# Seven block products for eight in the down projections and in five pairs of W_up columns of a two-layer encoder

## The chip, the cores and the metric

The kernel runs on one core of a Trainium2 chip. A core has TensorE (PE, matmuls; PEld is its weight load), VectorE (DVE), ScalarE (ACT), GpSimd (POOL), SyncE (SP, which issues most DMAs) and 16 DMA engines. Operands lie in SBUF with 128 partitions; matmuls add into PSUM, which has eight banks of 128 x 512 float32. Each engine works through its own instructions in order and waits on semaphores for others. The metric is the device time of one execution in microseconds (us).

## The reference

Two layers over x of 512 positions x 1024 channels, all in float32:

```
h   = RMSNorm(x);  p = h @ W_in            # Fourier group, q, k, v
x   = x + concat(RMSNorm(Fourier part), RMSNorm(windowed attention)) @ W_o
h   = RMSNorm(x)
up  = DWConv3_centred(h @ W_up)             # 2 x 2816 columns, 3 taps along positions, bias
x   = x + (silu(up[:, :2816]) * up[:, 2816:]) @ W_down
```

The last three lines are the ConvFFN, which the change rewrites. Its hidden width of 2816 is 22 blocks ("ff tiles") of 128.

## The kernel before

Channels lie on the partitions and the 512 positions on the free dimension, so x is eight tiles `x[0]` to `x[7]` of 128 x 512. Every operand of a matmul is split into a high part (`whi` for weights, written by ACT as a rounding copy) and a low part (`wlo`, written by DVE as the difference, L93). A product is three matmuls, high x high, low x high, high x low (`mm3`, L120 to L122), with a block of weights of 128 x 128 as the stationary operand and 512 positions as the moving one. `whi` and `wlo` have five buffers each, a raw weight tile (`wraw`) is loaded by SP.

The ConvFFN of a layer runs in two halves of 11 ff tiles (`HALVES`). For each ff tile the kernel makes two W_up tiles (gate and value): two weight splits of 512, 24 matmuls into one bank, then DVE multiplies the bank by the norm's factor (`tF<-ps,rb`), ACT takes the middle tap of the convolution, and DVE the two other taps (L96). ACT applies silu, and the gate's product is made on DVE in layer 0 and on POOL in layer 1; it is split into `gu`, held in buffers with the names slab, pT and m4. Then comes the down projection of the half: for each of the eight tiles of x 11 blocks x 3 matmuls of 512 into one bank, and one DVE addition x += bank. In the last half of layer 1 the last of the eight tiles is done in two pieces of 256 positions.

In layer 0's ConvFFN a generator (`presplit`) splits layer 1's remaining weights (44 pieces, of W_qkv, W_in, the Fourier weights and W_o) into high and low parts in `tA` buffers and stores them in DRAM (`kept`), from which layer 1 fetches them. `next(ahead)` in the loops lets it go on by one piece.

The code is written in the order of the computation; a scheduler that simulates the engines decides the order of the instructions on each engine when the program is built.

Of the kernel before, what the change touches and what calls it, by code (L numbers as in the profile page):

```python
# [37 lines left out]
def encoder_kernel(tc, t):
# [109 lines left out]

    def presplit(l):
# [15 lines left out]
        def cols(src, n, step):  # L165
            def load():
                raw = temp(1024, "m4")
                nc.sync.dma_start(raw[:, :n], src)
                return [raw[:, c:c + step] for c in range(0, n, step)]
            return load  # L170

        def prepare(kind, raw):
            if kind == "u":
                return fold_wu(raw)
            return fold_wf(raw) if kind == "f" else raw

        jobs = []
        for grp in (1, 0):
            for kk in range(KT // 2):
                jobs.append((cols(t["w_qkv"][l, grp, kk], 768, 384), [f"qkv{grp}{2 * kk + i}" for i in range(2)]))  # L180
        for kk in range(KT // 2):
            jobs.append((lambda kk=kk: load_wu(l, kk, temp(1024, "m4")), [f"u{2 * kk + i}" for i in range(2)]))
        for j in range(NF):
            jobs.append((lambda j=j: [load_wf(l, j, temp(1024, "m4"))], [f"f{j}"]))
        for half in range(2):
            for mp in range(KT // 2):
                jobs.append((cols(t["w_o"][l, half, :, mp * 1024:(mp + 1) * 1024], 1024, 512),
                             [f"o{half}{2 * mp + i}" for i in range(2)]))
        got = jobs[0][0]()
        for n, (_, keys) in enumerate(jobs):  # L190
            for i, key in enumerate(keys):
                keep(key, prepare(key[0], got[i]))
                if i == len(keys) - 1 and n + 1 < len(jobs):
                    got = jobs[n + 1][0]()
                yield
# [182 lines left out]
    for l in range(L):
# [325 lines left out]
        ahead = presplit(l + 1) if l < L - 1 else iter(lambda: 0, 1)  # L704
        for f0, nf in HALVES:
            gu = []
            for fi in range(f0, f0 + nf):
                ys_ = []
                n = fi - f0
                for z in range(2):  # L710
                    m = fi + z * FT
                    w = wchunks(t["w_up"][l, m], 1024)
                    nps[0] += 1
                    o = psum(FFN_BANKS[nps[0] % len(FFN_BANKS)])
                    for k in range(KT):
                        mm3(o, [q[:, (k % 4) * P:(k % 4 + 1) * P] for q in w[k // 4]], [h2[k][:, s, :] for s in range(2)],
                            k == 0, k == KT - 1)
                    u = temp(512, "tF")
                    tt(u, o, rb2, ALU.mult)
                    y = temp(512, "tF")  # L720
                    act(y, u, AF.Identity, scale=cw[:, l, 1, m:m + 1], bias=cb[:, l, m:m + 1])
                    stt(y[:, 1:], u[:, :-1], cw[:, l, 0, m:m + 1], y[:, 1:], ALU.mult, ALU.add)
                    stt(y[:, :-1], u[:, 1:], cw[:, l, 2, m:m + 1], y[:, :-1], ALU.mult, ALU.add)
                    ys_.append(y)
                    if (2 * n + z) % 3 == 2:
                        next(ahead)
                act(ys_[0], ys_[0], AF.Silu)
# [1 line left out]
                if n < 4:
                    a = pair("slab")  # L730
                elif n < 8:
                    if n % 2 == 0:
                        two = temp(2048, "pT", F32R).rearrange("p (n s q) -> p n s q", n=2, s=2)
                    a = two[:, n % 2]
                else:
                    a = pair("m4")
                split(a[:, 0, :], a[:, 1, :], ys_[0])
                gu.append(a)
            nxt = []
            for m in range(KT):  # L740
                next(ahead)
                next(ahead)
                w = []
                for c in range(0, nf, 8):
                    n = min(8, nf - c)
                    w += wchunks(t["w_down"][l, m, :, (f0 + c) * P:(f0 + c + n) * P], n * P)
                end = l == L - 1 and f0 + nf == FT
                nh = 2 if end and m == KT - 1 else 1
                for h in range(nh):
# [100 lines left out]
```

## Time and profile before

| | before |
|---|---|
| median of 3 runs | 1056.19 us (1055.73 to 1057.11) |
| the profiled execution | 1056.14 us, its span 1054.3 us, granted clock 0.999 |
| PE busy | 1038.2 us, 98% of the span |
| DVE busy | 726.8 us, 69% |
| ACT busy | 507.9 us, 48% |
| POOL busy | 90.8 us, 9% |
| ConvFFN of layer 0, 155 to 509 us | PE 354.00 of 354 us, DVE 264.77 |
| ConvFFN of layer 1, 685 to 1051 us | PE 366.00 of 366 us, DVE 236.50 |
| DMA | 140.03 MB, 133 GB/s in the mean |

An instruction's recorded duration is longer than its share of a busy engine, since neighbours overlap; the distance of two starts tells what one costs there. Releasers of waits are inferred from semaphore events.

### The profile page before, as it was taken

How to read it: one execution, taken by the hardware profiler on the slowest of the kernel's cores; microseconds unless marked ns; L12 is line 12 of the kernel's file. 1: busy time of each engine (PE TensorE's matmuls, PEld its weight loads, DVE VectorE, ACT ScalarE, POOL GpSimd, SP SyncE). 2: the span in 40 equal slices, each digit the busy share in tenths (PEclk: the TensorE clock that was granted, in tenths of full speed). 3: DMA queues.
4: the chain of work that ended last, by engine and by line, in shares of the span. 5: the costliest groups of instructions: out<-in, count | busy, mean ns of one | idle time of the engine just before them, and what ended most of it. 6: DMA issues, size and time to landing. Idle time of an engine off the chain costs nothing.

```text
span 1054.3 us, 14425 instructions
## 1 busy us (share of the span) xinstructions
PE 1038.2 (98%) x5107; PEld 873.2 (83%) x5107; DVE 726.8 (69%) x1384; ACT 507.9 (48%) x939; POOL 90.8 (9%) x164
## 2 busy tenths in 40 slices
PE   8998999999999999999999999999999999999998
PEld 8986778888888888888899887888888888888887
DVE  8878768697767777777519775478877336878632
ACT  5339755455444445455423785246554224454421
POOL 0004410000000000000000152001101000101100
PEclk9999999999999999999999999999999999999999
DMA  7232152332269833239856313333332333332241
GB/s 273 83 115 87 58 193 81 100 100 96 78 226 353 324 100 101 89 114 322 280 181 221 113 62 99 122 100 94 101 101 74 96 115 100 98 101 82 82 150 48
DMA packets 60475, 140.03 MB, mean 133 GB/s; under 512 B 6642, under 2 KB 22258, under 8 KB 60404
## 3 DMA queue, kind: packets, MB, share of 16 engines
q1 hardware_dynamic: 60404, 139.12, 40.5%
q8 instruction: 40, 0.66, 0.3%
q14 instruction: 31, 0.25, 0.1%
HBM read 116.02 MB, written 23.07 MB: 132 GB/s over the span
## 4 chain that ended last, share of the span: by engine, by line
PE 93%; DVE 2%; DMA 2%; ACT 1%; issue 1%; POOL 0%; SPq 0%; ACTq 0%; DVEq 0%; POOLq 0%
PE ps L122 28%; PE ps L120 28%; PE ps L121 28%; PE ps L118 3%; PE ps L548 2%; PE ps L541 2%; PE ps L529 1%; DMA wraw<-in_w_qkv_dram 1%; PE ps L234 1%; PE ps L227 1%; ACT tA L90 0%; DMA x<-in_xT_dram 0%; DVE tA L533 0%; ACT act L90 0%; PE ps L500 0%
## 5 line engine op out<-in xcount | busy, mean ns | idle before, releaser
L90 ACT ACTIVATE whi<-wraw 128x512 fp32r<-128x512 f32 (+1 forms) x296 | 182.0, 616 | 290.8 <-PE ps L122 278.4
L120 PE MATMUL ps<-act,whi 128*128 128x512 f32 x768 | 298.9, 390 | 0.0
L121 PE MATMUL ps<-act,wlo 128*128 128x512 f32 x768 | 298.3, 389 | 0.0
L122 PE MATMUL ps<-act,whi 128*128 128x512 f32 x768 | 298.2, 389 | 0.0
L93 DVE TENSOR_TENSOR wlo<-wraw,whi 128x512 fp32r<-128x512 f32 (+1 forms) x304 | 219.7, 726 | 103.4 <-ACT whi L90 102.0
L122 PEld LDWEIGHTS ps<-act,whi 128*128 128x128 f32 x768 | 144.2, 188 | 30.1
L120 PEld LDWEIGHTS ps<-act,whi 128*128 128x128 f32 x768 | 144.2, 188 | 29.7
L121 PEld LDWEIGHTS ps<-act,wlo 128*128 128x128 f32 x768 | 144.2, 188 | 29.7
L96 DVE SCALAR_TENSOR_TENSOR tF<-tF,pb,tF 128x511 f32<-128x511 f32 x176 | 133.5, 763 | 11.1 <-ACT tF L90 8.7
L93 DVE TENSOR_TENSOR tF<-ps,rb 128x512 f32<-128x512 f32 x104 | 71.2, 689 | 77.9 <-PE ps L122 64.7
L120 PE MATMUL ps<-slab,whi 128*128 128x512 f32 (+2 forms) x212 | 82.2, 388 | 0.0
L122 PE MATMUL ps<-slab,whi 128*128 128x512 f32 (+2 forms) x212 | 79.9, 380 | 0.4 <-DVE slab L93 0.3
L121 PE MATMUL ps<-slab,wlo 128*128 128x512 f32 (+2 forms) x212 | 80.0, 378 | 0.0
L90 ACT ACTIVATE tF<-tF,pb 128x512 f32<-128x512 f32 x88 | 71.7, 816 | 11.3 <-DVE tF L93 4.6
L93 DVE TENSOR_TENSOR x<-x,ps 128x512 f32<-128x512 f32 (+1 forms) x49 | 32.9, 674 | 36.5 <-PE ps L122 36.3
L93 POOL TENSOR_TENSOR tF<-tF,tF 128x512 f32<-128x512 f32 x22 | 30.2, 1371 | 256.1 <-DVE tF L96 224.1
L120 PE MATMUL ps<-pT,whi 128*128 128x512 f32 (+1 forms) x132 | 50.5, 383 | 0.0
L121 PE MATMUL ps<-pT,wlo 128*128 128x512 f32 (+1 forms) x132 | 50.5, 383 | 0.0
L122 PE MATMUL ps<-pT,whi 128*128 128x512 f32 (+1 forms) x132 | 50.5, 383 | 0.0
L538 POOL TENSOR_SCALAR tA<-tA,den 128x256 f32<-128x256 f32 (+1 forms) x64 | 37.4, 590 | 145.1 <-DVE den L537 144.6
L533 DVE CUSTOM_DVE_ANT_0 tA<-ps,pb,nsink 128x256 f32<-128x256 f32 (+1 forms) x64 | 37.8, 603 | 14.5 <-PE ps L529 9.7
L122 PEld LDWEIGHTS ps<-slab,whi 128*128 128x128 f32 x212 | 39.7, 188 | 8.3 <-DVE slab L93 0.9
(178 smaller groups left out, 1485.0 us busy)
## 6 DMA issues: line engine op xcount, KB each, us to landing
wraw<-in_w_up_dram SPq DMA_DIRECT2D x88, 512.0 KB, 3.5
wraw<-in_w_down_dram SPq DMA_DIRECT2D x32, 512.0 KB, 3.7
kept<-tA SPq DMA_DIRECT2D x56, 256.0 KB, 5.7
whi<-kept SPq DMA_DIRECT2D x28, 256.0 KB, 3.0
wlo<-kept SPq DMA_DIRECT2D x28, 256.0 KB, 3.0
kept<-tA SPq DMA_DIRECT2D x32, 192.0 KB, 4.4
wraw<-in_w_down_dram SPq DMA_DIRECT2D x32, 192.0 KB, 2.4
wraw<-in_w_o_dram SPq DMA_DIRECT2D x8, 512.0 KB, 3.7
```

The costliest lines, as they stand in the source:

```text
L90: return nc.scalar.activation(out, in_, func, **kw)
L93: return (eng or nc.vector).tensor_tensor(out, a, b, op=op)
L96: return nc.vector.scalar_tensor_tensor(out=out, in0=a, scalar=s, in1=b, op0=op0, op1=op1)
L118: nc.tensor.matmul(out, a[0], b[0], start=start, stop=stop, **kw)
L120: nc.tensor.matmul(out, a[0], b[0], start=start, stop=False, **kw)
L121: nc.tensor.matmul(out, a[1], b[0], start=False, stop=False, **kw)
L122: nc.tensor.matmul(out, a[0], b[1], start=False, stop=stop, **kw)
L227: nc.tensor.matmul(pt[:, 2 * b:2 * b + 2], acc[:, b * P:(b + 1) * P], ones2, start=True, stop=True)
L533: nc.vector.tensor_tensor_reduce(out=pr[:, :n], in0=sc[:, :n], in1=mask[:, m0:m0 + n], scale=qs_scale[p][:, i, e:e + 1], scalar=nsink[:, l ...
L538: nc.gpsimd.tensor_scalar(pr[:, :n], pr[:, :n], den[:, i:i + 1], 1.0, op0=ALU.mult, op1=ALU.mult)
L541: tr = nc.tensor.transpose(pp[:, j * P:(j + 1) * P], pr[:, j * P:(j + 1) * P], ident)
L548: pv = nc.tensor.matmul(py[64 * e:64 * e + 64, i0 * P:(i1 + 1) * P], vp[:, j, 64 * g:64 * g + 64], pT[:, half, e, b0:b0 + 2 * (i1 - i0) + ...
```

## The change

**Groups.** The ConvFFN of both layers runs in three groups of 6, 8 and 8 ff tiles (`GROUPS`) instead of two halves of 11.

**Down projection.** A pair of x tiles (rows 1 and 2 of a 2 x 2 block matrix) is made from two halves of the group's ff tiles (columns) and two halves of the 512 positions. Seven products of blocks take the place of eight. With A the weights and B the right operands, A's sums are S1 = A21 + A22, S3 = A11 - A21, S2 = S3 - A22, S4 = A12 + S2, and B's sums T1 to T4 (`sums_of_b`). Each product has kp blocks (3 or 4) x 3 matmuls of 256. They go to three banks: X gets B11, T2, T3 and T4 in turn, Y gets T1 and then B22, Z gets B21. A bank goes on adding; after each product DVE adds the whole bank to the part of x to which the sum so far belongs, and only then may the next product go on in the bank. The additions are seven of 256 a pair.

**Weight sums** are made by DVE (`wsum` in layer 0, `tA` in layer 1), except S1 of the first three pairs of a group, for which SP loads A21 and a DMA issued by POOL adds A22 to it (18 in all). All seven left operands of a pair are split into high and low parts.

**Right operands.** The ff tiles are made in the order in which the two of a pair follow each other. For a pair `seven_gu` makes four sums of 256 on DVE and splits 3.5 tiles of 512.

**W_up.** In layer 1 the pairs of W_up tiles with the numbers 4, 8, 11, 16 and 19 (`SEVEN`) are made by the same seven products (`up_seven`, 84 matmuls of 256 for 48 of 512), with sums of h2 that are made once (`seven_h`) in rooms that are free by then. Banks are read out between products by ACT and DVE.

**Others.** The gate's product is on DVE in both layers. The ConvFFN takes banks in a ring of eight (`BANKS8`) instead of six. `presplit` works in 44 jobs of one piece each; the high copies wait for the last convolution's first step (`pace`), and raw pieces lie in the `tail` buffers.

```diff
+GROUPS = [(0, 6), (6, 8), (14, 8)]
+SEVEN = ((), (4, 8, 11, 16, 19))
+BANKS8 = ("mm", "mm", "mm", "av", "sc", "sc", "tp", "tp")
...
         def keep(key, src):
             two = [temp(n, "tA", F32R) for _ in range(2)]
-            split(two[0], two[1], src)
+            with tc.issue_after(pace[0]):
+                act(two[0], src)
+            tt(two[1], src, f(two[0]), ALU.subtract)
...
+    def sums_of_b(b1, b2):
+        t13, t24 = temp(512, "tF"), temp(512, "tF")
+        tt(t13[:, LO], b1[:, HI], b1[:, LO], ALU.subtract)
+        tt(t13[:, HI], b2[:, HI], b1[:, HI], ALU.subtract)
+        tt(t24[:, LO], t13[:, LO], b2[:, HI], ALU.subtract)
+        tt(t24[:, HI], t24[:, LO], b2[:, LO], ALU.add)
+        return t13, t24
...
+    def seven_gu(b1, b2, room):
+        t13, t24 = sums_of_b(b1, b2)
+        one = next(room)
+        g = dict(B11=[one[:, LO], one[:, HI]])
+        split(*g["B11"], b1[:, LO])
+        parts(g, b2, ("B21", "B22"), room)
+        parts(g, t13, ("T1", "T3"), room)
+        parts(g, t24, ("T2", "T4"), room)
+        return g
...
+    def up_seven(l, fi, h2, ts, rb2):
...
+        product(X, wsplit(a11), "B11", True)
+        act(ua[:, LO], X)
+        s1, s2, s3, s4 = [temp(512, "tA") for _ in range(4)]
+        tt(s1, a21, a22, ALU.add)
+        product(Y, wsplit(s1), "T1", True)
+        act(ub[:, HI], Y)
+        product(Z, wsplit(a12), "B21", True)
+        tt(ua[:, LO], ua[:, LO], Z, ALU.add)
...
+        product(X, wsplit(s2), "T2")
+        act(ua[:, HI], X)
...
+        product(X, wsplit(a22), "T4")
...
+    def first_two(l, mp, f0, kp):
...
+        nc.sync.dma_start(s1, wd(l, 2 * mp + 1, f0, kp, 0))
+        nc.gpsimd.dma_start(s1, wd(l, 2 * mp + 1, f0, kp, 1), accum_op=ALU.add)
...
+        yield "X", wsplit(two_m[0][:, mp % 2 * 512:mp % 2 * 512 + n]), "B11", 0, 0, False
+        yield "Y", wsplit(s1), "T1", 1, 1, False
+
+    def other_five(l, mp, f0, kp, first):
...
+        s2, s3, s4 = [wroom(i, n) if l == 0 else temp(n, "tA") for i in (1, 2, 3)]
+        tt(s3, a11, a21, ALU.subtract)
+        tt(s2, s3, a22, ALU.subtract)
+        yield "X", wsplit(s2), "T2", 0, 1, False
+        yield "Z", wsplit(a12), "B21", 0, 0, True
+        yield "X", wsplit(s3), "T3", 1, 1, True
+        tt(s4, a12, s2, ALU.add)
+        yield "Y", wsplit(s4), "B22", 0, 1, True
+        yield "X", wsplit(a22), "T4", 1, 0, True
...
+            def products(mp, ws):
+                for b, w, key, r, c, landed in ws:
...
+                    for k in range(kp):
+                        mm3(o, [z[:, k * P:(k + 1) * P] for z in w], gu[k][key], k == 0 and key in ("B11", "B21", "T1"),
+                            k == kp - 1, skip_group_check=True)
+                    m, q0 = 2 * mp + r, 256 * c
+                    tt(x[m][:, q0:q0 + 256], x[m][:, q0:q0 + 256], o, ALU.add)
...
-                tt(ys_[0], ys_[0], ys_[1], ALU.mult, nc.gpsimd if l else nc.vector)
...
-                    for k in range(nf):
-                        mm3(o, [z[:, (k % 4) * P:(k % 4 + 1) * P] for z in w[k // 4]],
-                            [gu[k][:, s, q0:q1] for s in range(2)], k == 0, k == nf - 1)
-                    tt(x[m][:, q0:q1], x[m][:, q0:q1], o, ALU.add)
```

DVE's order in layer 0 before, from the last W_up product of the first half (`tF_645<-ps_644`) to the first addition to x; `wlo` is the low half of a weight, `tA<-m4` the low half of a piece of layer 1's weights:

```order
L93 TENSOR_TENSOR tF_645_2930<-ps_644_2905,rb_418_1893 128x512
L93 TENSOR_TENSOR wlo_679_3035<-wraw_675_3028,whi_678_3034 128x512
L96 SCALAR_TENSOR_TENSOR tF_646_2932<-tF_645_2930,pb_96,tF_646_2932 128x511 x2
L93 TENSOR_TENSOR wlo_682_3041<-wraw_680_3038,whi_681_3040 128x384
L93 TENSOR_TENSOR tF_634_2883<-tF_634_2883,tF_646_2932 128x512
L93 TENSOR_TENSOR m4_647_2938<-tF_634_2883,m4_647_2938 128x512
L93 TENSOR_TENSOR wlo_695_3100<-wraw_693_3097,whi_694_3099 128x512
L93 TENSOR_TENSOR tA_654_2952<-m4_652_2949,tA_653_2951 128x384
L93 TENSOR_TENSOR tA_667_3011<-m4_652_2949,tA_666_3010 128x384
L93 TENSOR_TENSOR tA_672_3021<-m4_670_3018,tA_671_3020 128x384
L93 TENSOR_TENSOR wlo_697_3104<-wraw_693_3097,whi_696_3103 128x512
L93 TENSOR_TENSOR x0_74<-x0_74,ps_665_2975 128x512
```

The same engine in the changed kernel, in the down projection of layer 0's first group, from the third product of the first pair of x tiles on (`ps_583` is that pair's bank X, `ps_584` its Y; `praw` is a piece of layer 1's weights):

```order
L95 TENSOR_TENSOR x0_74<-x0_74,ps_583_2562 128x256
L95 TENSOR_TENSOR tA_638_2778<-praw_631_2765,tA_637_2777 128x384
L95 TENSOR_TENSOR wlo_626_2723<-wsum_618_2689,whi_625_2722 128x384
L95 TENSOR_TENSOR wlo_628_2738<-wsum_619_2690,whi_627_2737 128x384
L95 TENSOR_TENSOR wlo_630_2752<-wraw_616_2683,whi_629_2751 128x384
L95 TENSOR_TENSOR tA_659_2871<-praw_636_2775,tA_658_2870 128x384
L95 TENSOR_TENSOR wsum_644_2792<-wraw_641_2785 128x384
L95 TENSOR_TENSOR x1_75<-x1_75,ps_583_2562 128x256
L95 TENSOR_TENSOR wsum_643_2791<-wsum_644_2792,wraw_642_2786 128x384
L95 TENSOR_TENSOR x0_74<-x0_74,ps_584_2573 128x256
L95 TENSOR_TENSOR tA_680_2964<-praw_657_2868,tA_679_2963 128x384
L95 TENSOR_TENSOR wsum_645_2793<-wraw_642_2786,wsum_643_2791 128x384
```

Where one addition to x stood among low halves of weights, there are now additions of half the width, weight sums and low halves in turn.

In layer 1, DVE's order before at the end of the first half (`m4` is the last tile's `gu`):

```order
L93 TENSOR_TENSOR m4_1755_7978<-tF_1746_7931,m4_1755_7978 128x512
L93 TENSOR_TENSOR wlo_1776_8086<-wraw_1774_8083,whi_1775_8085 128x512
L93 TENSOR_TENSOR wlo_1778_8090<-wraw_1774_8083,whi_1777_8089 128x512
L93 TENSOR_TENSOR x0_74<-x0_74,ps_1764_7997 128x512
L93 TENSOR_TENSOR wlo_1781_8096<-wraw_1779_8093,whi_1780_8095 128x384
L93 TENSOR_TENSOR wlo_1785_8137<-wraw_1783_8134,whi_1784_8136 128x512
```

In the changed kernel, at the end of layer 1's second group (`tF_2179` and `tF_2180` are the sums of the last pair of ff tiles, `tA` the weight sums, `ps_2184` and `ps_2185` banks X and Y of the first pair of x tiles):

```order
L95 TENSOR_TENSOR tA_2221_10196<-wraw_2218_10189,tA_2219_10194 128x512
L95 TENSOR_TENSOR m4_2181_9973<-tF_2164_9904,m4_2181_9973 128x512
L95 TENSOR_TENSOR tA_2236_10293<-wraw_2233_10286 128x512
L95 TENSOR_TENSOR tF_2180_9966<-tF_2180_9966,tF_2164_9904 128x256
L95 TENSOR_TENSOR m4_2182_9976<-tF_2179_9965,m4_2182_9976 128x512
L95 TENSOR_TENSOR m4_2183_9979<-tF_2180_9966,m4_2183_9979 128x512
L95 TENSOR_TENSOR x0_74<-x0_74,ps_2210_10122 128x256
L95 TENSOR_TENSOR x1_75<-x1_75,ps_2185_9996 128x256
L95 TENSOR_TENSOR x3_77<-x3_77,ps_2192_10035 128x256
L95 TENSOR_TENSOR x5_79<-x5_79,ps_2200_10076 128x256
L95 TENSOR_TENSOR x0_74<-x0_74,ps_2184_9982 128x256
L95 TENSOR_TENSOR wlo_2212_10137<-tA_2204_10097,whi_2211_10136 128x512
```

The single low half of the last ff tile has become a chain of sums and three low halves, and five additions of 256 to x stand together before the next low half of a weight.

More of the change, by code (lines that the diff above doesn't have):

```diff
@@ L163, in store, with room @@
                 late.pop()()
[L165 to L175, printed above, removed]
+        def room():
+            return tp.tile([P, 516], F32, tag="tail", name=nm("praw"), bufs=2)[:, :512]
@@ L177, in presplit, with load @@
+        def load(src):
+            raw = room()[:, :src.shape[-1]]
+            nc.sync.dma_start(raw, src)
+            return raw
         jobs = []
         for grp in (1, 0):
[L179 to L182, printed above, removed]
+            for k in range(KT):
+                c = (k % 2) * 384
+                jobs.append((f"qkv{grp}{k}", t["w_qkv"][l, grp, k // 2, :, c:c + 384]))
@@ L183, in presplit @@
+        for k in range(KT):
+            jobs.append((f"u{k}", t["w_in"][l, k * P:(k + 1) * P, 0:FW]))
         for j in range(NF):
-            jobs.append((lambda j=j: [load_wf(l, j, temp(1024, "m4"))], [f"f{j}"]))
+            jobs.append((f"f{j}", j))
         for half in range(2):
[L186 to L195, printed above, removed]
+            for m in range(KT):
+                jobs.append((f"o{half}{m}", t["w_o"][l, half, :, m * 512:(m + 1) * 512]))
+        def begin(key, src):
+            return load_wf(l, src, room()) if key[0] == "f" else load(src)
@@ new lines, in parts, with h_rooms @@
+    def parts(g, src, keys, room):
+        two = [next(room), next(room)]
+        split(*two, src)
+        for key, cols in zip(keys, (LO, HI)):
+            g[key] = [z[:, cols] for z in two]
+    def h_rooms():
+        for tag in ("th0", "th1", "tl0", "tl1", "wt0", "wt1", "v", "accA", "accF"):
+            yield cp.tile([P, 512], F32R, tag=tag, name=nm("room"), bufs=1)
+        z = sp.tile([P, 1024], F32R, tag="ropetab", name=nm("room"), bufs=1)
+        yield from (z[:, :512], z[:, 512:])
+        for _ in range(2):
+            yield tp.tile([P, 516], F32R, tag="tail", name=nm("room"), bufs=2)[:, :512]
+        for _ in range(2):
+            yield temp(512, "sq", F32R)
+        yield cp.tile([P, 512], F32R, tag="room", name=nm("room"), bufs=1)
@@ new lines, in seven_gu, with up_eight @@
+    def seven_gu(b1, b2, room):
[4 more added lines that the diff above has]
+        parts(g, b2, ("B21", "B22"), room)
+        parts(g, t13, ("T1", "T3"), room)
+        parts(g, t24, ("T2", "T4"), room)
+        return g
+    def up_eight(l, fi, h2, ts, rb2):
+        for z in range(2):
+            w = wchunks(t["w_up"][l, fi + z * FT], 1024)
+            o = third()
+            for k in range(KT):
+                mm3(o, [q[:, (k % 4) * P:(k % 4 + 1) * P] for q in w[k // 4]], [h2[k][:, s, :] for s in range(2)],
+                    k == 0, k == KT - 1)
+            u = temp(512, "tF")
+            tt(u, o, rb2, ALU.mult)
+            yield u
@@ new lines, in conv, with gate, wd @@
+    def conv(l, m, u):
+        y = temp(512, "tF")
+        pace[0] = act(y, u, AF.Identity, scale=cw[:, l, 1, m:m + 1], bias=cb[:, l, m:m + 1]).ins
+        stt(y[:, 1:], u[:, :-1], cw[:, l, 0, m:m + 1], y[:, 1:], ALU.mult, ALU.add)
+        stt(y[:, :-1], u[:, 1:], cw[:, l, 2, m:m + 1], y[:, :-1], ALU.mult, ALU.add)
+        return y
+    def gate(ys):
+        act(ys[0], ys[0], AF.Silu)
+        tt(ys[0], ys[0], ys[1], ALU.mult)
+    def wd(l, m, f0, kp, half):
+        return t["w_down"][l, m, :, (f0 + half * kp) * P:(f0 + (half + 1) * kp) * P]
@@ L703, in encoder_kernel @@
             tabs, alts, wt = load_tables(1)
[L704 to L727, printed above, removed]
-                tt(ys_[0], ys_[0], ys_[1], ALU.mult, nc.gpsimd if l else nc.vector)
[L729 to L749, printed above, removed]
-                    q0, q1 = h * S // nh, (h + 1) * S // nh
-                    nps[0] += 1
-                    o = psum(FFN_BANKS[nps[0] % len(FFN_BANKS)])[:, q0:q1]
-                    for k in range(nf):
-                        mm3(o, [z[:, (k % 4) * P:(k % 4 + 1) * P] for z in w[k // 4]],
-                            [gu[k][:, s, q0:q1] for s in range(2)], k == 0, k == nf - 1)
-                    tt(x[m][:, q0:q1], x[m][:, q0:q1], o, ALU.add)
-                    if end:
-                        nc.sync.dma_start(t["out"][m, :, q0:q1], x[m][:, q0:q1])
-                if l < L - 1 and f0 + nf == FT:
-                    nxt.append(norm_tile(m, g1[:, l + 1, :], acc))
-            xg = nxt
```

109 lines of the change are left out of this document (107 added, 2 removed).

## The prediction

> **What bounds the kernel now.** I read the page's busy times first, then its slices, the windows of the two ConvFFN stages, and last single instructions on TensorE (PE), VectorE (DVE) and ScalarE (ACT).
>
> ```profile
> span 1054.3 us, 14425 instructions
> PE   1038.2 (98%) x5107; PEld 873.2 (83%) x5107; DVE 726.8 (69%) x1384; ACT 507.9 (48%) x939; POOL 90.8 (9%) x164
> ...
> PE   8998999999999999999999999999999999999998
> ...
> DVE  8878768697767777777519775478877336878632
> ...
> PEclk9999999999999999999999999999999999999999
> ```
>
> PE is busy for 98% of the span, at the full granted clock, and has no slice of idle time. So time comes off only if PE has less to do, and goes on wherever PE has to wait. The stages that the change rewrites are these (the first line of numbers is layer 0's ConvFFN, the second layer 1's):
>
> ```profile
> core 0: us, PE busy (x) PEld busy (x) DVE busy (x) ACT busy (x) POOL busy (x), PEclk, DMA share, GB/s
> 155.00:509.00 354.00, 354.00 (x1575) 293.45 (x1574) 264.77 (x430) 178.42 (x282) 1.70 (x2) 1.00 0.49 166
> 685.00:1051.00 366.00, 366.00 (x1654) 304.51 (x1652) 236.50 (x327) 152.54 (x234) 31.17 (x23) 1.00 0.31 96
> ```
>
> PE never stops there: 354.00 of 354 and 366.00 of 366 us. DVE is second with 265 (75%) and 237 (65%), ACT has half, the DMA engines half or less.
>
> **What PE saves.** Its matmuls overlap, so their price is the distance of two starts and not the duration. The kernel's last down tile already runs 256 wide:
>
> ```profile
> start us, us, engine line op out<-in xcount [idle before <-releaser]
> 1041.62 0.39 PE L120 MATMUL ps<-m,whi 128*128 128x512 f32 x1
> ...
> 1042.98 0.28 PE L120 MATMUL ps<-slab,whi 128*128 128x256 f32 x1
> ...
> 1050.78 0.28 PE L122 MATMUL ps<-m,whi 128*128 128x256 f32 x1
> ```
>
> Between the first two starts lie six matmuls of 512: 1.36/6 = 0.227 us each. Between the second and the third lie 65 of 256: 7.80/65 = 0.120 each, a little more than half. Down projection of a layer: before 8 tiles x 22 blocks x 3 = 528 of 512, 119.7 us; after 4 pairs of tiles x 7 products x 11 blocks x 3 = 924 of 256, 110.9 us; 8.8 less, 17.6 in both layers. Each pair of W_up that is changed: 48 of 512 (10.88) become 7x4x3 = 84 of 256 (10.08), 0.8 less, 4.0 for five. The last down tile was 66 x 0.120 = 7.9 where 512-wide ones would have cost 7.5; that 0.4 also goes. PE has 22 us less. With no new wait the profiled execution of 1056.14 (its span plus 1.8; the median of the runs is 1056.19, so I use 1056.1) would become 1034.
>
> **What it adds on DVE.** DVE too overlaps neighbours, so again I take start distances:
>
> ```profile
> 334.52 0.75 DVE L93 TENSOR_TENSOR tA<-m 128x255 f32<-128x255 f32 x2
> 335.19 0.68 DVE L93 TENSOR_TENSOR x<-x,ps 128x512 f32<-128x512 f32 x1
> 335.79 0.69 DVE L93 TENSOR_TENSOR wlo<-wraw,whi 128x512 fp32r<-128x512 f32 x1
> 336.39 0.69 DVE L93 TENSOR_TENSOR tA<-tA,tA 128x512 fp32r<-128x512 f32 x1
> ...
> 290.73 0.55 DVE L93 TENSOR_TENSOR wlo<-wraw,whi 128x384 fp32r<-128x384 f32 x1
> 291.20 1.54 DVE L96 SCALAR_TENSOR_TENSOR tF<-tF,pb,tF 128x511 f32<-128x511 f32 x2
> ...
> 718.86 2.73 DVE L96 SCALAR_TENSOR_TENSOR tF<-tF,pb,tF 128x511 f32<-128x511 f32 x4
> 721.50 0.69 DVE L93 TENSOR_TENSOR wlo<-wraw,whi 128x512 fp32r<-128x512 f32 x1
> ```
>
> Back to back a tensor-tensor of 512 takes 0.60 us, of 384 0.47, of 256 0.335 (two in 0.67), a conv step 0.66 (2.64/4). PE got half the columns for half the price plus 6%; DVE pays 12% more, and has more to do. Per layer:
> - sums of the right operands, 4 x 256 for each of 11 pairs: 44 x 0.335 = 14.7.
> - their low halves: 22 of 512 before, 33 of 512 and 11 of 256 now: +10.3.
> - x += bank: 16 of 512 (9.6) become 3 groups x 4 pairs x 7 = 84 of 256 (28.1): +18.5.
> - weight sums: 13 of 384 and 26 of 512: +21.7 (the S1 of three pairs in four goes to accumulating DMAs).
> - low halves of the weights: 32 of 512 and 16 of 384 (26.7) become 56 of 512 and 28 of 384 (46.7): +20.
>
> That is 85 us in layer 0. Layer 1 has them too, and the gate's 22 multiplications, which leave POOL (22 x 0.60 = 13.2), the sums of h2 (10.2), and in each W_up pair of the seven kind four weight sums, three more low halves and about one more addition (5.3 each, 26.4): 135 us. DVE gets 220 us for PE's 22.
>
> Spread evenly that would nearly fit. But DVE works in order, and PE needs its results at places. So I counted in the changed instruction order, at six places, DVE's work from a row that must wait for a PE product to a row that PE must wait for (the low half of a weight, or the emptying of a bank), and PE's work between those same two points. Where DVE's is longer, PE stands still for the difference, whatever ACT and the DMAs do.
>
> 1. Layer 0, group 1, from the last W_up product to the x3 addition that frees X of the second pair: 6 of 512, 27 of 384, 20 of 256, 5 conv steps = 26.2; PE 135 of 256 = 16.2. Stall 10.0.
> 2. Layer 0, group 2, from the first x0 addition to the low half of a weight sum in the second round: 30 of 512, 29 of about 256, 2 conv steps and 6 small ones = 29.8 (the split of layer 1's weights is 8 of it); PE 159 of 256 = 19.1. Stall 10.7.
> 3. Layer 0, group 3, from the last W_up product to a late low half, with layer 1's first norm tiles: 49, 27 of 256, 7 conv steps = 43.0; PE 301 of 256 = 36.1. Stall 6.9.
> 4. Layer 1, from the first W_up product over the h2 sums and the first pair of seven: 52, 16 of 384, 44 of 256, 24 conv steps = 69.2; PE 169 of 512, 159 of 256 and 8 small = 58.2. Stall 11.0.
> 5. and 6. Layer 1, groups 2 and 3, transition: 31, 18 of 256, 10 conv steps = 31.2; PE 60 of 512 and 99 of 256 = 25.5. Stall 5.7 each.
>
> No two overlap, so they add: 230.6 of DVE against 180.7 of PE, 50 us. This is a lower bound at these prices, since DVE has waits of its own inside. A transition shows them:
>
> ```profile
> 273.20 0.69 DVE L93 TENSOR_TENSOR tF<-ps,rb 128x512 f32<-128x512 f32 x1 [1.36 <-PE ps L122]
> 273.87 0.69 DVE L93 TENSOR_TENSOR wlo<-wraw,whi 128x512 fp32r<-128x512 f32 x1
> 274.79 1.54 DVE L96 SCALAR_TENSOR_TENSOR tF<-tF,pb,tF 128x511 f32<-128x511 f32 x2 [0.22 <-ACT tF L90]
> 276.59 0.69 DVE L93 TENSOR_TENSOR wlo<-wraw,whi 128x512 fp32r<-128x512 f32 x1 [0.27 <-ACT whi L90]
> 277.20 0.69 DVE L93 TENSOR_TENSOR tF<-tF,tF 128x512 f32<-128x512 f32 x1
> ...
> 277.92 0.63 ACT L90 ACTIVATE m<-tF 128x512 fp32r<-128x512 f32 x1 [1.36 <-DVE tF L93]
> ```
>
> From the product to the gate's end DVE has 0.5 us of idle time, and it hands to ACT and back once; after the change it does so for the sums as well. I take the 0.5 doubled and the dependent pair's extra 0.13 (1.54 against 2 x 0.66 + 0.09) some three times, about 1.3 a place, 8 us for six; ends 0 and 20 (DVE pausing 1.36 twice a place, as it does above for PE).
>
> **The rest.** ACT gets 162 instructions, some 0.63 us each, 102 us spread over two stages in which it has 390 idle: nothing, unless it is late behind DVE (in the 8 us). POOL loses 22 of its 164 instructions and gets 18 accumulating DMAs. No such DMA is in this trace. The nearest rows are the plain ones:
>
> ```profile
> wraw<-in_w_down_dram SPq DMA_DIRECT2D x32, 512.0 KB, 3.7
> ...
> kept<-tA SPq DMA_DIRECT2D x56, 256.0 KB, 5.7
> ...
> wraw<-in_w_down_dram SPq DMA_DIRECT2D x32, 192.0 KB, 2.4
> ```
>
> Such a DMA starts only behind the load of the first half: at least 2.4 + 2.4. The sum is needed after one product of 36 to 48 matmuls (4.3 to 5.8 us), or later. Ends: 0, since it is issued ahead in the last W_up tile, and 5.7 - 2.4 = 3.3 for each of 18, 59 us, were none ahead and no DVE stall in the same place. I take 0, nearest to the 3.7 and 2.4 of loads, which DVE's stall covers; were that cover gone, some 3 us in each of six groups, 18, would show. SP issues 95 DMAs more; at a DMA share of 0.49 and 0.31 I price them at 0 (upper end: in the 18). The split of layer 1's weights goes on piece by piece with the same pieces: 0 in sum, its work counted in places 1 to 3.
>
> The sum: 1056.1 - 22 + 50 + 8 = 1092.
>
> **A rule against the row.** The row: two tensor-tensors of 512 start 0.60 apart and each is recorded as 0.69 long. By the durations (0.69 for 512, 0.55 for 384, 0.75 - 0.335 = 0.42 for 256, 1.54/2 = 0.77 for a conv step) the six places hold 271 us of DVE work, not 231, and the stalls are 90. The Trainium skill, "VectorE: DVE Perf Modes", section "The DRAIN you can't avoid", says that the next operation does not start until the pipe has emptied. By that rule the result would be 1124; the trace, with starts 0.60 apart, does not agree, and its number stands in my sum.
>
> **The rivals.**
> - *Faster: PE's count decides.* 1034. For it: PE alone carries the present time, DVE's mean load after the change is still below PE's. It needs DVE to run ahead at the six places. It decides once DVE's work there is 12% shorter than at my spacings: 0.88 x 230.6 = 203, stalls 22, as much as PE saves. Against it: the spacing of 0.60 holds in every dense stretch that I read. Chance 0.10; no change at all (the balance hit within 0.2%) 0.03.
> - *Half the stalls*: some DVE work that I count as between the points turns out cheaper: 1056 - 22 + 25 + 4 = 1063; 0.10.
> - *DVE at its durations*, because most of its added work is in dependent chains and behind ACT: 1124; 0.12.
> - *The accumulating DMAs come late* as well: 1092 + 18 = 1110; 0.05.
>
> **How the numbers follow.** My forecast, 1075 to 1108 around 1092, has 0.60. Runs of this kernel lie within 1055.7 to 1057.1, so 0.2% (2 us) is about what can be told from no change. Slower: 0.60 + 0.10 + 0.12 + 0.05 = 0.87; same 0.03; faster 0.10. The range, 1063 to 1120, leaves out the faster case, no change and the upper part of the durations' case, about 2 in 10.
>
> **What would show it.** PE's busy time should fall by about 22 us, and its idle time, now none in these stages, should appear at the six places, released by DVE (wlo, x, or the parts of gu), 5 to 11 us each. DVE should be near 9 in the slices of the down projections. 256-wide matmuls should start 0.12 apart where PE doesn't wait. I am wrong if DVE's spacing is shorter than 0.55 for 512, if PE is still 97% busy, or if PE's idle time is released by a DMA.

## The result, and the profile after

The changed kernel takes 1138.97 us (median of 4 runs, 1135.15 to 1140.36) against 1056.09: a ratio of 1.078, 95% interval 1.075 to 1.081. The sign was forecast, the size was not: 83 us slower instead of 36. The profiled execution took 1137.70.

The head of its page, and the slices that answer to those of before:

```profile
span 1135.9 us, 17246 instructions
PE 1062.9 (94%) x6046; PEld 928.1 (82%) x6046; DVE 912.5 (80%) x1902; ACT 580.4 (51%) x1101; POOL 77.1 (7%) x160
...
PE   7999999988999899998999999994899998999988
...
DVE  7867747898799996988939673869798879888896
...
PEclk9999999998999999999999999996899998999989
```

PE is busy 94% of a longer span. Two things in these lines go against the forecast's picture. PE's busy time rose by 25 us, though it has 22 us less to do at the old prices; and the row of the granted clock, all nines before, has slices of 8 and one of 6. The clock fell.

The three groups of layer 0 and of layer 1, each window from one group's W_up to the next (the third window also holds layer 1's attention). Columns: length of the window, busy time of each engine, granted clock:

```profile
core 0: us, PE busy (x) PEld busy (x) DVE busy (x) ACT busy (x) POOL busy (x), PEclk, DMA share, GB/s
202.79:297.34 94.55, 86.34 (x465) 74.86 (x464) 83.57 (x166) 49.67 (x91) 2.67 (x3) 0.93 0.62 187
297.34:434.89 137.55, 131.22 (x719) 114.60 (x717) 123.34 (x241) 69.56 (x115) 2.57 (x3) 0.98 0.64 200
434.89:751.23 316.34, 305.61 (x1791) 266.99 (x1790) 233.79 (x510) 162.90 (x333) 31.15 (x69) 0.99 0.48 151
751.23:859.39 108.16, 88.62 (x510) 78.34 (x509) 95.43 (x189) 58.77 (x101) 2.69 (x3) 0.87 0.30 87
859.39:996.79 137.40, 130.59 (x782) 116.13 (x780) 115.19 (x207) 66.19 (x110) 2.60 (x3) 0.96 0.37 109
996.79:1132.20 135.41, 128.61 (x772) 114.47 (x770) 114.56 (x206) 65.12 (x107) 2.61 (x3) 0.96 0.36 106
```

PE's idle time in them is 8.2, 6.3, 10.7, 19.5, 6.8 and 6.8 us, 58 in all, of which 4 lie in the attention and were there before. So the pauses came out about as large in sum as forecast (50 + 8), and in about the forecast places; only the fourth window is far above its 11. The rest of the loss is inside PE's busy time.

It begins at the transition of layer 0's first group. PE's rows (start, duration, the wait ahead):

```profile
start us, us, engine line op out<-in xcount [idle before <-releaser]
250.59 0.38 PE L122 MATMUL ps<-pT,whi 128*128 128x256 f32 x1 [2.37 <-ACT pT L92]
...
251.28 0.28 PE L123 MATMUL ps<-pT,wlo 128*128 128x256 f32 x1
252.68 1.01 PE L124 MATMUL ps<-pT,whi 128*128 128x256 f32 x3 [1.12 <-DVE pT L95]
254.64 0.58 PE L122 MATMUL ps<-slab,whi 128*128 128x256 f32 x1 [0.96 <-ACT whi L92]
...
257.55 0.41 PE L122 MATMUL ps<-pT,whi 128*128 128x256 f32 x1
257.76 0.41 PE L123 MATMUL ps<-pT,wlo 128*128 128x256 f32 x1
257.98 0.41 PE L124 MATMUL ps<-pT,whi 128*128 128x256 f32 x1
```

The granted clock of two windows there (the last columns are clock, DMA share, GB/s):

```profile
251.50:252.00 0.50, 0.06 (x1) 0.00 (x0) 0.50 (x2) 0.00 (x0) 0.00 (x0) 1.00 0.35 101
252.00:252.50 0.50, 0.00 (x0) 0.00 (x0) 0.50 (x2) 0.00 (x0) 0.00 (x0) 0.61 0.81 194
```

The clock falls to half at about 252.1 us, inside the second pause, behind one of 2.37. When PE has nothing more to wait for, at 257.5, matmuls of 256 start 0.213 us apart where they took 0.120. No pause of 3 us is needed here. In layer 1, inside a pair of seven, two shorter ones do it:

```profile
911.77 0.50 PE L122 MATMUL ps<-act,whi 128*128 128x512 f32 x1 [0.72 <-ACT whi L92]
913.41 0.39 PE L122 MATMUL ps<-room,whi 128*128 128x256 f32 x1 [1.13 <-ACT tF L92]
```

The window with these 1.85 us of idle time is followed by one at about half clock:

```profile
911.00:913.50 2.50, 0.65 (x3) 0.28 (x2) 2.50 (x5) 2.28 (x5) 0.00 (x0) 1.00 0.00 0
914.00:917.50 3.50, 3.50 (x15) 3.09 (x14) 3.50 (x8) 1.80 (x4) 0.00 (x0) 0.54 0.39 139
```

PE fully busy, at a clock of 0.54. In windows of half a microsecond the clock is at half in twelve stretches whose lengths are multiples of about 3.4 us (3.4, 6.8, 10.2, one of 20.5), and PE's busy time lost in them (busy time x (1 - clock), summed) is 31 us: 28 in the ConvFFNs and 3 at the kernel's start. The kernel before has no such stretch until its last matmul. The Trainium skill, "TensorE: Matmul & The Clock Gate", section "HAM oscillation — how this bites in real kernels", gives the rule that PE must have no idle gap above some 3.4 us, or its clock falls to half. The half rate agrees with this trace; the size of the gap that brings it does not, since 0.72 and 1.13 us close together were enough. What exactly decides stays open: the kernel before has single pauses of 1.46 and 1.11 us (at 26.9 and 87.5 us) with no half clock behind them.

The fourth place, where PE waits for the sums of h2 (`room` is a split sum), in PE's waits of the whole execution (us in total, how many, the longest):

```profile
engine line waited for: us in total, times, longest us
PE ps L122 <- ACT room L92: 14.5, 2, 8.3
PE ps L122 <- ACT whi L92: 13.7, 17, 2.4
PE ps L123 <- DVE wlo L95: 6.7, 12, 1.4
```

and in two windows of the same columns as above:

```profile
780.00:790.00 10.00, 1.38 (x3) 0.79 (x3) 9.96 (x18) 7.03 (x12) 0.00 (x0) 0.50 0.02 7
790.00:800.00 10.00, 7.63 (x34) 6.94 (x34) 8.09 (x19) 5.55 (x11) 0.00 (x0) 0.59 0.01 2
```

From 780 to 790 us DVE works without a gap and PE 1.4 us of 10. ACT ends the two long waits, but its copies into `room` themselves wait for DVE's sums (0.64 and 1.06 us). Over the six windows without the attention ACT ended 39 us of PE's idle time and DVE 15; the forecast had named DVE.

Against PE's matmuls at full clock (0.227 and 0.120, counted in the instruction order between the same anchors), the loss is 3.8 us up to layer 0's ConvFFN, then 16.9, 11.1 and 13.5 in layer 0's groups, 29.0, 14.6 and 14.6 in layer 1's: 103.4 before rounding. Less 22 that is 81.4; the profiled executions differ by 81.6.

### The profile page after: what moved, and what is told of

The parts are those of the page before. It is cut to its first block, busy times and chain, and to the rows that moved or that the text cites. A ratio compares the mean times of both kernels' runs of the same rounds, so it can differ in the third digit from the quotient of the medians.

```text
span 1135.9 us, 17246 instructions
## 1 busy us (share of the span) xinstructions
PE 1062.9 (94%) x6046; PEld 928.1 (82%) x6046; DVE 912.5 (80%) x1902; ACT 580.4 (51%) x1101; POOL 77.1 (7%) x160
## 4 chain that ended last, share of the span: by engine, by line
PE 75%; DVE 14%; DMA 5%; ACT 3%; issue 2%; SPq 0%; POOL 0%; DVEq 0%; ACTq 0%; POOLq 0%
PE ps L123 22%; PE ps L122 22%; PE ps L124 22%; PE ps L120 3%; DVE wlo L95 3%; DMA wraw<-in_w_down_dram 2%; DVE tF L95 2%; DVE tF L98 2%; DVE tA L95 2%; PE ps L778 2%; PE ps L771 1%; PE ps L759 1%; DVE x L95 1%; DMA praw<-in_w_o_dram 1%; ACT whi L92 1%
## 5 line engine op out<-in xcount | busy, mean ns | idle before, releaser
L122 PE MATMUL ps<-act,whi 128*128 128x512 f32 (+1 forms) x748 | 286.2, 383 | 2.9 <-ACT whi L92 2.9
L123 PE MATMUL ps<-act,wlo 128*128 128x512 f32 (+1 forms) x748 | 285.9, 383 | 0.5 <-DVE wlo L95 0.5
L124 PE MATMUL ps<-act,whi 128*128 128x512 f32 (+1 forms) x748 | 285.4, 383 | 0.0
L95 DVE TENSOR_TENSOR x<-x,ps 128x256 f32<-128x256 f32 (+1 forms) x184 | 78.0, 438 | 34.4 <-PE ps L124 33.4
L122 PE MATMUL ps<-slab,whi 128*128 128x256 f32 (+2 forms) x272 | 87.5, 340 | 13.2 <-ACT whi L92 10.8
L123 PE MATMUL ps<-slab,wlo 128*128 128x256 f32 (+2 forms) x272 | 88.4, 326 | 6.7 <-DVE wlo L95 6.2
L95 DVE TENSOR_TENSOR tF<-ps,rb 128x512 f32<-128x512 f32 (+1 forms) x99 | 66.0, 673 | 32.6 <-PE ps L124 19.5
L124 PE MATMUL ps<-slab,whi 128*128 128x256 f32 (+2 forms) x272 | 85.7, 317 | 0.4 <-DVE slab L95 0.3
L122 PE MATMUL ps<-pT,whi 128*128 128x256 f32 x264 | 78.7, 299 | 3.7 <-ACT pT L92 3.7
L123 PE MATMUL ps<-pT,wlo 128*128 128x256 f32 x264 | 78.3, 298 | 0.0
L123 PEld LDWEIGHTS ps<-slab,wlo 128*128 128x128 f32 x272 | 54.2, 199 | 13.2 <-DVE wlo L95 10.9
L124 PE MATMUL ps<-pT,whi 128*128 128x256 f32 x216 | 63.6, 298 | 1.1 <-DVE pT L95 1.1
L124 PE MATMUL ps<-m,whi 128*128 128x256 f32 x208 | 58.8, 298 | 3.8 <-DVE m L95 3.8
```

The lines of the kernel that those rows point to most:

```text
L95: return (eng or nc.vector).tensor_tensor(out, a, b, op=op)
L122: nc.tensor.matmul(out, a[0], b[0], start=start, stop=False, **kw)
L123: nc.tensor.matmul(out, a[1], b[0], start=False, stop=False, **kw)
L124: nc.tensor.matmul(out, a[0], b[1], start=False, stop=stop, **kw)
```

## The experiments

**Parts of the change.** The whole change stands at 1139.0 us. *no_up7*: `SEVEN = ((), ())`, no pair of seven in W_up.

> The changed kernel without seven products in W_up (no pair of W_up, no sums of h2); both down projections stay with seven. Theory (VectorE is late at the places where PE needs it, and each group of short pauses is followed by some 3.4 to 7 us at half the granted clock): PE loses 16 us of pauses at the first such pair of layer 1, 5 us in the other four and about 7 us at half clock there; it gains these and gives back 4 us of matmuls: 1139 - 28 + 4 = about 1115. Rival (the seven products of W_up are the whole trouble): below 1056, since the down projections alone would save 18. Rival (they cost nothing): 1143.

Measured: 1098.9 us, ratio 1.039 (1.038 to 1.041). The five pairs cost 40 us and not 24. Their windows show where:

```profile
751.03:837.46 86.43, 84.72 (x475) 73.61 (x473) 79.06 (x154) 45.78 (x79) 2.67 (x3) 0.98 0.39 113
837.46:965.12 127.66, 126.18 (x710) 110.43 (x708) 106.74 (x185) 60.57 (x98) 2.60 (x3) 1.00 0.40 116
965.12:1091.50 126.38, 124.21 (x700) 108.68 (x698) 105.99 (x184) 59.16 (x95) 0.00 (x0) 1.00 0.33 101
```

Beside the last three windows of the changed kernel these are 21.7, 9.7 and 9.0 us shorter, although PE has 4 us more to do. Without the pairs the transitions of layer 1 hardly pause and the clock stays at 0.98 to 1.00. The transitions of groups 2 and 3, which the prediction counted at 5.7 us each (places 5 and 6), pause 4.0 and 3.4 us in the changed kernel and some 1.5 us each here: most of it comes with the pairs of seven.

*l0_only*, *l1_only*: the ConvFFN with seven products in one layer, the code of before in the other.

```diff
-SEVEN = ((), (4, 8, 11, 16, 19))
+SEVEN = ((), ())
...
-        xg = conv_ffn(l, h2, rb2, presplit(l + 1) if l < L - 1 else nothing)
+        xg = (conv_ffn if l == 0 else conv_old)(l, h2, rb2, presplit(l + 1) if l < L - 1 else nothing)
```

This is l0_only; l1_only has `l == 1` in place of `l == 0`.

> Seven products only in layer 0's down projection; layer 1 as before (eight products, two halves, gate on POOL). The piecewise split of layer 1's weights stays. Theory: the stretch up to layer 1's W_up keeps what it lost in the changed kernel, 36 us, and layer 1 is as before: 1056 + 36 = about 1092. Rival (only layer 1 costs, layer 0 has room on VectorE): 1047.

> Seven products only in layer 1's down projection, none in W_up; layer 0 as before with eight products and two halves, but with the piecewise split of layer 1's weights in it. Theory: 45 us lost in layer 1 less the 24 of the W_up pairs: 1056 + 21 = about 1077. If the piecewise split itself costs, layer 0 grows by that, and PE shows pauses between 155 and 520 us; theory: it doesn't (0 to 3).

Measured: 1092.8 (1.034, 1.033 to 1.036), as expected, and 1071.4 (1.013, 1.012 to 1.015), 6 us better than expected. Layer 0's part of the change (groups, piecewise split and seven products together) costs 36 us, layer 1's down projection some 6 on top of that (1098.9 - 1092.8). In l1_only 3.9 us of pauses and 4.7 us of half clock lie before layer 1's ConvFFN, at the norm tiles (695 to 709 us), where no other kernel has them; layer 0's ConvFFN, with the piecewise split in it, has none.

*groups*: `HALVES = [(0, 6), (6, 8), (14, 8)]` in the kernel before.

> The kernel before with three groups of 6, 8 and 8 ff tiles in place of two halves of 11, and nothing else. Theory: with eight products VectorE has time at one more transition; x is added to in 16 more steps of 0.6 us that lie beside PE work: 1056 to 1058. Rival (the transition itself is what costs): two transitions more at 6 us or more each plus the half clock, about 1075.

Measured: 1066.1 (1.009, 1.007 to 1.010). Neither: the transition is not free even with eight products. Layer 0's first one has four pauses (0.52, 0.45, 1.68, 1.56 us) and 3.4 us at half clock, W_up one of 0.73; the start of the kernel, where PE waits 2.0 us for the first norm, is followed by 6.8 us of half clock, and some 3 of the 10 us are there before the ConvFFN begins. Each profiled execution here but that of the kernel before loses 1.4 to 3.1 us to the half clock at the kernel's start; in the changed kernel it is 2.7 of the 3.8 us.

**What sets the pauses.**

*no_up7_nosums*: no weight sums on DVE; *no_bsums*: no sums of the right operands. The edit of no_up7_nosums:

```diff
-            tt(s1, a21, a22, ALU.add)
+            s1 = a21
...
-        tt(s3, a11, a21, ALU.subtract)
-        tt(s2, s3, a22, ALU.subtract)
+        s3, s2 = a21, a22
...
-        tt(s4, a12, s2, ALU.add)
+        s4 = a12
```

and of no_bsums:

```diff
-        t13, t24 = sums_of_b(b1, b2)
+        t13, t24 = b1, b2
```

> As no_up7, with the weight sums of VectorE left out (one block stands in the place of each sum, so the output is another); the sums by accumulating DMAs stay. VectorE has 78 instructions less, 43 us. Counted as in the prediction, its excess over PE at the six places falls from 37 to 21 us. Theory (VectorE's work at these places sets the pauses): 16 us less and 5 of half clock less: about 1078. Rival (ScalarE, whose work stays, or the turnaround of the banks sets them): 1095 or more.

> As no_up7, with the sums of the right operands left out (the two unsummed ff tiles are split in their place, so the output is another). VectorE has 88 instructions of 256 less, 29 us, less than the 43 us that no_up7_nosums took away for 7 us of time; but these stand in the chain from the last W_up product of a group to its first complete product. Theory (the chain at the transition counts, not the sum of VectorE's work): 12 us or more less than 1098.9, about 1086. Rival (VectorE's sum counts): 29/43 of 7 us, 1094.

Measured: 1092.2 (1.033, 1.032 to 1.035) and 1085.9 (1.027, 1.025 to 1.029). Taking 43 us of work from DVE gave 6.7 us, taking 29 us gave 13.0. The prediction's count, done again for no_up7_nosums, had 16 us of pauses less; it is refuted as a measure of gains, and so is DVE's work in sum. 1092.2 lies between the theory (1078) and its rival (1095). For no_bsums the theory on record, 1086, was met: the chain from the last W_up product to the first finished product of the down projection counts, in which the sums of the right operands stand. That weight sums cost less because they can run ahead is a reading of the order, not tested.

*no_up7_ahead2*: no split of layer 1's weights in the down projections.

```diff
                 next(ahead)
+                next(ahead)
                 gate(ys)
...
             for mp in range(3):
-                next(ahead)
                 products(mp, first_two(l, mp, f0, kp) if mp else ready)
             for mp in range(KT // 2):
-                next(ahead)
-                if mp == 1:
+                if f0 + nf == FT and mp == 0:
                     next(ahead)
```

The first `next(ahead)` added is the second piece of a W_up pair; the one that is left in the down projection comes when all 44 pieces are split.

> As no_up7, but no piece of layer 1's weights is split in the down projections of layer 0: two pieces a W_up pair instead of one, so the same work lies where VectorE has room. Counted as in the prediction, the excess at the three places of layer 0 falls from 28 to 17 us. Theory: 10 us of pauses and some 4 of half clock less: about 1085. Rival (the place of the split doesn't matter): 1099.

Measured: 1089.8 (1.031, 1.029 to 1.033), 9 us less than no_up7. The chain of no_up7 at the first transition (start, duration, what) shows what such a piece does there; `praw` is the raw piece:

```profile
250.04 2.85 DMA praw<-in_w_qkv_dram
252.91 0.53 ACT tA L92
...
261.91 3.04 DMA praw<-in_w_qkv_dram
265.04 0.53 ACT tA L92
...
266.02 2.56 DMA praw<-in_w_qkv_dram
```

and ACT's rows there:

```profile
252.91 0.52 ACT L92 ACTIVATE tA<-praw 128x384 fp32r<-128x384 f32 x1 [3.19 <-DMA praw<-in_w_qkv_dram]
253.34 0.51 ACT L92 ACTIVATE whi<-wsum 128x384 fp32r<-128x384 f32 x1
```

ACT's copy of a piece waits 3.19 us for a load, and the high half of a weight sum, which PE wants, stands behind it in ACT's queue, though DVE's last sum before it was done at 247.6 us. Three loads of 2.5 to 3 us lie in this one transition. ACT's waits for such loads in no_up7:

```profile
ACT tA L92 <- DMA praw<-in_w_o_dram: 9.0, 4, 4.3
ACT tA L92 <- DMA praw<-in_w_qkv_dram: 7.6, 4, 3.2
```

and in no_up7_ahead2:

```profile
ACT tA L92 <- DMA praw<-in_w_qkv_dram: 0.6, 1, 0.6
```

The prediction counted such a piece as 0.47 us of DVE and nothing on ACT. The run takes both away at once, and its forecast of 14 us, from DVE's work alone, is not far from the 9 measured. So the rows show the loads in ACT's queue, but how the 9 us divide between them and DVE's work is not shown.

*no_up7_ahead2_pool*: three low halves of seven on POOL (`wsplit(a12, nc.gpsimd)` and two more).

> As no_up7_ahead2, with three of the seven low halves of a pair of x tiles (B21, B22, T4) made by POOL, which takes some 1.3 us each against VectorE's 0.6. The count of the excess falls from 27 to 17 us. Theory: 1085 - 10 - 5 = about 1070. Rival (POOL's slower instructions come late for PE, or slow VectorE beside them): 1085 or more.

Measured: 1105.7 (1.046, 1.044 to 1.047), the rival. POOL took 1.49 us in the mean for the low half of a raw weight and 3.95 for one of 384 at the first transition, for which PE waited 3.5; DVE's additions to x, for which PE waited 2.2 us in no_up7_ahead2, come late too (PE's waits):

```profile
PE ps L122 <- DVE x L95: 9.4, 9, 1.9
PE ps L123 <- POOL wlo L95: 8.5, 7, 3.5
```

*no_up7_noacc*: without the line that issues the accumulating DMA.

> As no_up7, without the 18 accumulating DMAs of POOL (the second block is missing in S1 of three pairs in four, so the output is another). Theory (they land in time): 1096 to 1099; what the start of the kernel loses beside them may come back, 3 us. Rival of the prediction (they come late, 18 us in six groups): about 1081.

Measured: 1097.5 (1.039, 1.037 to 1.040): the accumulating DMAs cost nothing that shows.

**The half clock.** Fillers in the unused half of the banks:

```diff
                         mm3(o, [z[:, k * P:(k + 1) * P] for z in w], gu[k][key], k == 0 and key in ("B11", "B21", "T1"),
                             k == kp - 1, skip_group_check=True)
+                        for _ in range(fill[0] + (k == kp - 1) * fill[1]):
+                            nc.tensor.matmul(spare, w[0][:, :P], gu[0][key][0], start=True, stop=True, skip_group_check=True)
```

> As no_up7 (1098.9), with matmuls that compute nothing of use in the unused half of the banks at each transition: 2 of 256 after each block of the first six products of a group and 6 behind each of the next products of the first pair, 66 to 78 a group (8 to 9 us). They give PE something to do where it would pause. Theory (short pauses bring the half clock, which costs no_up7 13 us of PE work in the ConvFFNs): the granted clock stays nearer to 1 and the time falls although PE has 50 us more to do: 1086 to 1095. Rival (the half clock is no consequence of the pauses, PE's load is what counts): 1110 to 1145.

> As no_up7_fill, but with 18 to 24 matmuls of 256 a group, in layer 0 only (one after each block of the first six products; 66 in all, 8 us of PE); the output is another, since the additional matmuls disturb the banks' sums. It tells whether the half clock costs time of its own. If it does (PE at 0.213 a matmul is then the last to be ready): the clock stays up in layer 0 and the time falls by some 5 to 10 us against no_up7's 1098.9: 1089 to 1094. If the work of VectorE and ScalarE sets the pace there and PE at half rate only waits less: 1097 to 1101, with less half clock and more pauses.

Measured: 1115.8 (1.055, 1.053 to 1.057) and 1100.4 (1.041, 1.040 to 1.042). The window from layer 0's W_up to layer 1's, first in no_up7:

```profile
202.06:751.03 548.97, 523.12 (x2969) 456.61 (x2968) 441.06 (x915) 282.25 (x539) 38.98 (x78) 0.98 0.55 171
```

in no_up7_fill:

```profile
203.88:754.80 550.92, 537.62 (x3191) 474.97 (x3190) 441.81 (x915) 283.66 (x539) 39.96 (x78) 0.99 0.56 171
```

and in fill_light:

```profile
203.57:751.97 548.40, 525.06 (x3036) 460.30 (x3034) 440.63 (x915) 281.61 (x539) 40.06 (x78) 0.98 0.56 172
```

With no_up7_fill the granted clock rose from 0.984 to 0.994 over the execution, as the theory had it, but the time lies in the rival's range. In layer 0 the fillers (222 more matmuls, 26.6 us) cost 2.0 us and what the half clock takes from PE there fell from 11.8 to 3.4 us, yet nothing was gained: PE's pauses and slow matmuls were filled, and the other engines' pace stayed. In layer 1, which hardly paused, the same 26.6 us cost 15.5. The light filler's 8 us cost nothing (-0.6), and 7.6 us of half clock stayed. So in layer 0 the loss at half clock overlaps the lateness of the others at least in part; fillers that also run where PE doesn't pause can't say how much.

Where PE is the bound it is otherwise. Pauses put into the kernel before:

```diff
+LUMP = (3, 6, 14, 18)
...
+                    if l == 1 and fi in LUMP and z == 0:
+                        raw = wload(t["w_up"][l, m], 1024)
+                        d, late_w = temp(512, "sq"), temp(512, "tA")
+                        tt(d, u, u, ALU.subtract)
+                        for _ in range(6):
+                            tt(d, d, d, ALU.add)
+                        tt(late_w, raw[:, :512], d, ALU.add)
+                        w = [wsplit(late_w), wsplit(raw[:, 512:])]
```

`d` is zero, once the product before is read. This is pause_long; in pause_short the loop has `range(0)`.

> The kernel before with four pauses put in: in layer 1 the weights of four W_up tiles (ff tiles 3, 6, 14, 18) are split only after VectorE has read the product before (a difference of zero is added to the first half of the weights). Everything else is as before, so PE is the bound again right behind each pause. The chain (reading the bank 0.7, two more VectorE steps 1.4, ScalarE's high copy 0.7) lets PE pause some 2.5 to 3 us four times, less where it has another tile's work: at most 12 us, 1056 + 12 = 1068 with the full clock. Theory (the half clock is time of its own where PE is the bound): on top of the pauses the time grows by 1.7 us for each 3.4 us at half clock, up to 7 us: 1068 to 1075. Rival (the half clock costs nothing of its own): the growth equals the pauses.

> As pause_short with six VectorE steps more in each chain (0.6 to 0.8 us each, 4.2 in sum): pauses of some 7 us, at most 28 in sum. Theory: the half clock starts behind each, 3.4 to 6.8 us long, and adds 1.7 to 3.4 each: 1056 + 28 + 7 to 14 = 1091 to 1098, less what other tiles' work takes off the pauses. Rival: growth equal to the pauses, 1084 at most.

Measured: 1085.1 (1.026, 1.024 to 1.027) and 1110.2 (1.049, 1.048 to 1.051). The pauses were longer than I expected (6.1 and three of 3.5; 13.1 and three of 9.8), so the totals miss; the question is answered by the window of layer 1's ConvFFN, first in the kernel before:

```profile
714.88:1050.80 335.92, 335.92 (x1516) 279.49 (x1514) 216.37 (x293) 140.29 (x213) 30.16 (x22) 1.00 0.31 96
```

in pause_short:

```profile
716.64:1078.80 362.16, 345.26 (x1516) 284.42 (x1514) 217.68 (x302) 139.22 (x214) 33.86 (x22) 0.98 0.29 89
```

and in pause_long:

```profile
716.01:1104.30 388.29, 345.81 (x1516) 284.60 (x1514) 234.83 (x326) 139.55 (x214) 30.94 (x22) 0.94 0.27 83
```

The same 1516 matmuls keep PE busy for 335.92, 345.26 and 345.81 us: 9.3 and 9.9 us more, for four pauses, and that comes on top of 16.9 and 42.5 us of idle time. Behind a pause of 3 us in pause_short:

```profile
771.02 0.50 PE L121 MATMUL ps<-act,whi 128*128 128x512 f32 x1 [2.95 <-ACT whi L91]
772.06 0.80 PE L121 MATMUL ps<-act,whi 128*128 128x512 f32 x1 [0.54 <-ACT whi L91]
772.65 0.63 PE L122 MATMUL ps<-act,wlo 128*128 128x512 f32 x1
773.08 0.63 PE L123 MATMUL ps<-act,whi 128*128 128x512 f32 x1
```

0.43 us from start to start instead of 0.227, for 3.4 us. The half clock is time of its own there. By the granted clock it takes 1.5 to 1.7 us behind each pause of 3.5 us, 1.9 to 2.7 behind each of 9.8, and 2.7 and 2.2 behind the longest one of either kernel: a pause three times as long does not pay three times as much.

**The five pairs.** *seven_late*: `SEVEN = ((), (11, 16, 19))`. *no_hsums*: the unsummed parts of h2 in place of T1 to T4; ACT's copies for the sums go with them.

```diff
-        b = [temp(512, "tF") for _ in range(2)]
-        for i in range(2):
-            act(b[i], x[k + 4 * i], scale=g2[:, l, k + 4 * i:k + 4 * i + 1])
...
-        t13, t24 = sums_of_b(*b)
-        parts(g, t13, ("T1", "T3"), room)
-        parts(g, t24, ("T2", "T4"), room)
+        g.update(T1=g["B11"], T3=g["B21"], T2=g["B22"], T4=g["B22"])
```

> The changed kernel with three of the five W_up pairs by seven products (11, 16, 19), so that the first of them stands in the second group and not behind the fourth pair of layer 1; the sums of h2 are made at the same place, but are needed seven pairs later. Theory (at the first pair PE waits because the sums of h2, their splits and the pair's weight sums crowd on VectorE, while ordinary pairs leave it 2 us each): group 1 of layer 1 falls back to what no_up7 has there, 22 us less than in the changed kernel, group 2 has one such pair less (5 us), two pairs give back 1.6: 1139 - 22 - 5 + 2 = about 1114. Rival (each pair of seven costs the same wherever it stands, a fifth of 40): 1139 - 16 = 1123.

> The changed kernel with the sums of h2 and their splits left out (unsummed parts of h2 stand in their places, so the output is another); the five pairs of seven and their weight sums stay. Theory (10 us of VectorE, 16 low halves and copies of it and of ScalarE, crowd before the first pair): layer 1's group 1 falls from 29 us of loss to about 10, the other groups keep their 14.6: 1139 - 19 = about 1120. Rival (the pair itself, its weight sums and the turnaround of its bank cost the 29): 1135 or more.

Measured: 1120.9 (1.061, 1.058 to 1.063), between the theory (1114) and its rival (1123), and 1127.0 (1.066, 1.064 to 1.068), again between. With the first pair moved, layer 1's first group still loses 16.9 us (29.0 in the changed kernel, 6.5 in no_up7): the sums of h2 push the end of the group late, and PE waits 6.9 us in one piece for the last right operand. Without the sums of h2 it loses 19.7. Less the 6.5 of no_up7, the sums of h2 alone cost the first group 10.4 us, the pair alone 13.2, and both together 22.5: here the two nearly add. The pairs of groups 2 and 3 cost about 5 us each.

None of the kernels beat the one before.

## Why the prediction was wrong

- **The matmuls' price held.** The 256-wide matmuls start 0.12 apart where PE neither waits nor runs slow, and the matmul sums close the account (103.4 - 22 = 81.4 against 81.6).
- **DVE's price held.** It is 0.60 and 0.335 us back to back, so the rival at the durations (1124) was not at work, near as its number comes to 1139.
- **The sum of the pauses held by chance in part.** 58 us were forecast and 54 more than before were measured. Layer 0's three places gave 8, 6 and about 7 us of idle time for 10.0, 10.7 and 6.9. Place 4 gave 16.0 for 11, and 3.5 more stand at the first transition of layer 1, for which the forecast had no place: the count looked for PE's needs among weights and banks, and left out the right operands that DVE and ACT split (`room`, `pT`, `m`), which is what PE's rows wait for there. Places 5 and 6 gave 4.0 and 3.4 for 5.7 each, and shrink to some 1.5 without the pairs of seven; the two pairs in each of these groups take 2.8 us more. The waits were forecast to be released by DVE; ACT ended 39 of the 55 us. A lower bound between two rows told where PE would stop; it did not tell what an edit is worth, as the two kernels without sums show.
- **The failed step: "PE has 22 us less".** The sum priced every matmul at the full clock that before shows, and had no term for what the pauses do to it. PE's busy time was forecast to fall by 22 us and rose by 25. Of these 47 us, 31 are read as half clock (3 of them at the start). The other 16 are what is left over. They are matmuls that start late without as much idle time in the rows, since a row of 256 lasts 0.28 us where its share is 0.12: between the starts at 251.28 and 252.68 lie 1.40 us, of which 1.12 are shown as idle. That is read from the rows and not tested.
- **The split of layer 1's weights was mis-sized.** It was costed as DVE's work, with nothing for ACT. Moved out of the transitions it gave 9 us; the rows show loads of some 3 us ahead of weights in ACT's queue, but the share of DVE's work in the 9 us is not shown.
- **Right:** the accumulating DMAs do not come late (no_up7_noacc).

What stays open: how much of the half clock in layer 0 is time of its own, what the 16 us beside it consist of, and how layer 0's 36 us divide. So the term that failed is shown, and its size where PE is the bound; its share of the 47 us in the changed kernel is argued.

## What to carry to other kernels

When an edit trades a saturated engine's time for work on its neighbours, cost the pauses twice: once as idle time and once, as an upper end, as the half clock behind them, 1.7 us for each 3.4 us stretch here; pauses of about a microsecond close together were enough. Then look not at the neighbour's total load but at the chain that opens each phase, and at every in-order queue in which something that waits for a load stands ahead of something that PE needs. Fewer matmuls on the bound engine did not pay here, and getting the right operands' sums out of that chain would not have been enough: no_up7 without them still took 1085.9 us.
